# A causal convolution's set-up: sums formed while transposing on TensorE, two weights made off VectorE, and another order

## Chip, cores and metric

One core of one Trainium2 chip. The metric is the time of one execution on the device in microseconds; a number quoted for a kernel is the median of its runs. A kernel is called faster or slower when it differs by more than 2%, and "same" within that. Each experiment was timed in three rounds beside the kernel before on the same chip. The experiments ran on several chips; the kernel before had medians of 796.1 to 796.8 us on all of them, which links the sessions: the changed kernel was timed in another one. Where I set an experiment against it, I give the difference of the medians; by the two ratios to the kernel before, it comes out within 0.8 us of that.

## The reference

```python
# x [8, 4096, 512], kernel [8, 512, 512], both float32, drawn with a fixed seed
def reference(x, kernel):
    out = np.zeros_like(x)
    for k in range(8):
        shifted = x if k == 0 else concatenate([zeros(B, k, D), x[:, :-k, :]], axis=1)
        out += np.matmul(shifted, kernel[k])
    return out
```

Every output row is the sum of eight earlier rows of x, each times its own 512x512 matrix.

## The kernel before

The time axis is cut into 128 runs, one for each partition, and every run is computed in steps of 8 rows. A step needs its 8 rows of x and the 7 rows before them. Done directly it would be 64 products of a row with a tap (one of the eight 512x512 matrices). The kernel uses a three-level scheme with fewer products: each step has three nodes, LO, HI and MID, and each node has nine products of four matmuls of 128x512: three first ones, two called V and four called L. The price is that sums of rows (the "streams" D4, D41, D42, D421; for the MID node D1, D2, D21) and differences of weights are needed. There are 8 loaded weights and 19 differences, written W[a, b, c] with MID in one or more places.

```python
    def mid_a(b_, c_): tt(W[MID, b_, c_], W[HI, b_, c_], W[LO, b_, c_], SUB)   # tt is VectorE
    def mid_b(a, c_):  tt(W[a, MID, c_], W[a, HI, c_], W[a, LO, c_], SUB)
    def mid_c(a, b_):  tt(W[a, b_, MID], W[a, b_, LO], W[a, b_, HI], SUB)
```

In the steady state x is transposed by DMA. The first step is prepared by another way, and this is what the change touches: the rows of x and of history are transposed on TensorE, copied out by ScalarE, and then summed on VectorE. "History" is the 7 rows ahead of each run, taken from the run before.

```python
    nc.vector.memset(D421, 0.0)                     # history goes into D421
    xi = [load_x(0, 0)]                             # rows 0..3 of x
    for b in range(B):                              # eight history loads
        nc.gpsimd.dma_start(out=D421[b * G + 1:(b + 1) * G, 1:8],
                            in_=xr[b * G:(b + 1) * G - 1, RUN - 7:RUN, :])
    for tap in (6, 4, 7, 5):
        load_w(tap)
    xi.append(load_x(0, 1))                         # rows 4..7 of x
    for tap in (2, 0, 3, 1):
        load_w(tap)
    ...
        transpose_pe(T, xi[0], range(0, 4))         # 16 matmuls of 128x128
        transpose_pe(H, D421, range(0, 8))          # 32
        nc.scalar.copy(out=XT[:, 0:4], in_=T[:, 0:4])
        ...
        nc.scalar.copy(out=hs, in_=H[:, 4:8])
        tt(D4[:, 5:8], H[:, 1:4], hs[:, 1:4], ADD)  # first stream
        tt(D4[:, 0:4], hs, XT[:, 0:4], ADD)
        ...
        transpose_pe(T, xi[1], range(4, 8))         # the second half of x
        nc.scalar.copy(out=XT[:, 4:8], in_=T[:, 4:8])
        tt(F1[:, 0], hs[:, 3], XT[:, 0], ADD)       # third stream: six sums
        ...
        tt(F21, F2[:, 0:4], F2[:, 1:5], ADD)
        ...                                         # D4, D41, D42, D421 of HI
    ...                                             # 8 zero-fills of PSUM
    nodes = [node_a1(*order[0])]                    # the first large product
    node_a0u(nodes[0]); node_seed(nodes[0])
    node_v(nodes[0], 0); node_v(nodes[0], 1)        # V products and "corrections"
    for k, (i, a) in enumerate(order):
        node_l(cur, 0, LO); node_l(cur, 0, HI)      # L products
        ...
            if k == 0:  # five differences for the second node
                mid_b(HI, HI); mid_c(HI, LO); mid_b(HI, LO); mid_c(HI, MID); mid_c(HI, HI)
            else:       # nine differences for the third node
                mid_a(LO, HI); mid_a(HI, HI); mid_b(MID, HI); mid_a(LO, LO); mid_a(HI, LO)
                mid_b(MID, LO); mid_c(MID, MID); mid_c(MID, LO); mid_c(MID, HI)
```

(Cuts are marked with dots; calls are joined on one line here to save room.) The correction is one VectorE operation after each V product; the L products of a node can only start after it. A node's two corrections are therefore good landmarks: first, second and third corrections are those of the LO, HI and MID node of the first step.

Of the kernel before, what the change touches and what calls it, by code (L numbers as in the profile page):

```python
# [18 lines left out]
LO, HI, MID = 0, 1, 2  # L19
# [3 lines left out]
def kernel(  # L23
# [6 lines left out]
    nc = tc.nc  # L30
    B, S, D = x.shape
# [21 lines left out]

    ctx.enter_context(tc.manual_schedule())

    ident = spool.tile([P, P], bf, name="ident")
    make_identity(nc, ident)
    zero = spool.tile([P, D], bf, name="zero")
    nc.vector.memset(zero, 0.0)

    W = {}
    for a in (LO, HI, MID):
        for b_ in (LO, HI, MID):
# [9 lines left out]
    D21 = spool.tile([P, 4, D], bf, name="D21")  # L73
    D1 = spool.tile([P, 2, D], bf, name="D1")

    F2 = spool.tile([P, 5, D], bf, name="F2")
    F21 = spool.tile([P, 4, D], bf, name="F21")
    F1 = spool.tile([P, 2, D], bf, name="F1")
    F0 = spool.tile([P, D], bf, name="F0")
# [1 line left out]
    def tt(o, a, b, op):  # L81
        nc.vector.tensor_tensor(out=o, in0=a, in1=b, op=op)  # L82


    def load_x(i, h):
        xin = xpool.tile([P, 4, D], bf, name="xin")
        nc.gpsimd.dma_start(out=xin, in_=xr[:, K * i + 4 * h:K * i + 4 * h + 4, :])  # L87
        return xin
# [15 lines left out]
    def prep_d27():  # L104
        tt(D2[:, 0], XT[:, 5], XT[:, 7], ADD)
# [26 lines left out]



    nc.vector.memset(D421, 0.0)  # L135
    xi = [load_x(0, 0)]
    for b in range(B):
        nc.gpsimd.dma_start(out=D421[b * G + 1:(b + 1) * G, 1:8],
                            in_=xr[b * G:(b + 1) * G - 1, RUN - 7:RUN, :])

    def load_w(tap):
        n = K - 1 - tap
        nc.gpsimd.dma_start(out=W[n >> 2, n >> 1 & 1, n & 1], in_=kr[:, :, tap, :])  # L143

    def mid_a(b_, c_):
        tt(W[MID, b_, c_], W[HI, b_, c_], W[LO, b_, c_], SUB)

    def mid_b(a, c_):
        tt(W[a, MID, c_], W[a, HI, c_], W[a, LO, c_], SUB)

    def mid_c(a, b_):
        tt(W[a, b_, MID], W[a, b_, LO], W[a, b_, HI], SUB)

    for tap in (6, 4, 7, 5):
        load_w(tap)
    xi.append(load_x(0, 1))
    for tap in (2, 0, 3, 1):
        load_w(tap)

    with tc.tile_pool(name="t", bufs=1, space=PSUM) as tpool:  # L160
        H = tpool.tile([P, K, D], bf, name="hist")
        T = tpool.tile([P, K, D], bf, name="xt0")

        def transpose_pe(o, src, ts_):
            for t in ts_:
                for c in range(DC):
                    nc.tensor.transpose(o[:, t, c * P:(c + 1) * P],  # L167
                                        src[:, t % src.shape[1], c * P:(c + 1) * P], ident)

        transpose_pe(T, xi[0], range(0, 4))  # L170
        transpose_pe(H, D421, range(0, 8))
        nc.scalar.copy(out=XT[:, 0:4], in_=T[:, 0:4])
        nc.scalar.copy(out=F0, in_=T[:, 0])
        hs = D421[:, 4:8]
        nc.scalar.copy(out=hs, in_=H[:, 4:8])  # L175
        tt(D4[:, 5:8], H[:, 1:4], hs[:, 1:4], ADD)
        tt(D4[:, 0:4], hs, XT[:, 0:4], ADD)
        prep_d41(LO)
        mid_b(LO, HI)
        tt(D42[:, 7], D4[:, 5], D4[:, 7], ADD)  # L180
        prep_d42(LO)
        mid_c(LO, LO)
        prep_d421(LO)
        mid_b(LO, LO)
        mid_c(LO, MID)
        mid_c(LO, HI)
        transpose_pe(T, xi[1], range(4, 8))
        nc.scalar.copy(out=XT[:, 4:8], in_=T[:, 4:8])  # L188
        tt(F1[:, 0], hs[:, 3], XT[:, 0], ADD)
        tt(F1[:, 1], XT[:, 0], XT[:, 1], ADD)  # L190
        tt(F2[:, 0], hs[:, 1], hs[:, 3], ADD)
        tt(F2[:, 1:3], hs[:, 2:4], XT[:, 0:2], ADD)
        tt(F2[:, 3:5], XT[:, 0:2], XT[:, 2:4], ADD)
        tt(F21, F2[:, 0:4], F2[:, 1:5], ADD)
        prep_d4(HI)
        prep_d41(HI)
        prep_d42(HI)
        prep_d421(HI)
        prep_d27()
    xi = [load_x(1, 0), load_x(1, 1)]  # L200


    ppool = ctx.enter_context(tc.tile_pool(name="p", bufs=3, space=PSUM))
    qpool = ctx.enter_context(tc.tile_pool(name="q", bufs=1, space=PSUM))
    for k in range(4):
        pw = ppool.tile([P, 2, D], f32, name="pp") if k else qpool.tile([P, 2, D], f32, name="qq")
        for h in range(2):
            nc.tensor.matmul(pw[:, h], lhsT=ident, rhs=zero, start=True, stop=True)  # L208

    mpool = ctx.enter_context(tc.tile_pool(name="m", bufs=2))  # L210
    cpool = ctx.enter_context(tc.tile_pool(name="c", bufs=2))
# [12 lines left out]
    def streams(i, a):  # L224

        if a == MID and i == 0:
            return (F0, [F1[:, 0], F1[:, 1]], [F2[:, 1], F2[:, 3]],
                    [F21[:, j] for j in range(4)])
        if a == MID:
            return (XT[:, 0], [D1[:, 0], D1[:, 1]], [D2[:, 1], D2[:, 3]],  # L230
                    [D21[:, j] for j in range(4)])
        o = 4 * a
        return (D4[:, o], [D41[:, 2 * a], D41[:, 2 * a + 1]], [D42[:, o], D42[:, o + 2]],
                [D421[:, o + j] for j in range(4)])
# [4 lines left out]



    def node_a1(i, a):
        n = Node()
        n.i, n.a, n.s = i, a, streams(i, a)
        n.q = qpool.tile([P, 2, D], f32, name="qq")
        product(n.q[:, 1], n.s[1][1], W[a, MID, HI], True)
        nc.scalar.copy(out=n.q[:, 0], in_=n.q[:, 1])  # L247
        n.p = {}
        return n
# [4 lines left out]

    def node_seed(n):
        for b_ in range(2):
            n.p[b_] = ppool.tile([P, 2, D], f32, name="pp")
            if b_ == LO:
                nc.scalar.copy(out=n.p[b_][:, 1], in_=n.q[:, 1])  # L259
            else:  # L260
                nc.scalar.mul(out=n.p[b_][:, 1], in_=n.q[:, 1], mul=-1.0)  # L261
        n.dts = cpool.tile([P, D], f32, name="dts")
        nc.scalar.copy(out=n.dts, in_=n.q[:, 0])  # L263
# [40 lines left out]

    order = [(0, LO), (0, HI), (0, MID)]
    order += [(i, a) for i in range(1, NIT) for a in (MID, LO, HI)]
    nodes = [node_a1(*order[0])]
    node_a0u(nodes[0])
    node_seed(nodes[0])
    node_v(nodes[0], 0)  # L310
    node_v(nodes[0], 1)
    for k, (i, a) in enumerate(order):
        cur = nodes[k]
        stage = k % 3
# [5 lines left out]
        if k < 2:  # L320
            node_l(cur, 1, LO)
            node_l(cur, 1, HI)
            node_e(cur, 0)
            if k == 0:
                mid_b(HI, HI)
                mid_c(HI, LO)
                mid_b(HI, LO)
                mid_c(HI, MID)
                mid_c(HI, HI)
                nodes.append(node_a1(*order[1]))  # L330
            else:
                mid_a(LO, HI)
                mid_a(HI, HI)
                mid_b(MID, HI)
                mid_a(LO, LO)
                mid_a(HI, LO)
                mid_b(MID, LO)
                mid_c(MID, MID)
                mid_c(MID, LO)
                mid_c(MID, HI)  # L340
                nodes.append(node_a1(*order[2]))
            node_e(cur, 1)
        nxt = nodes[k + 1] if k + 1 < len(order) else None
        if nxt:
            node_a0u(nxt)
# [26 lines left out]
            prep_d4(LO if stage == 1 else HI)  # L372
        if k >= 2:
            node_l(cur, 1, HI)
        if 1 <= k and k + 2 < len(order):
            nodes.append(node_a1(*order[k + 2]))
        if k >= 2:
            node_e(cur, 1)
        if stage == 1 and more:
# [33 lines left out]
```

## Time and profile before

| | before |
|---|---|
| runs | 795.45, 796.1, 798.13 us |
| profiled span | 793.6 us |
| first correction starts | 38.55 us |
| second | 48.16 us |
| third | 61.89 us |
| from about 63 us | TensorE always busy, 7.78 us a node |

The page's line of busy times is the first thing to read; it gives for each engine the busy microseconds, the share of the span, and the number of instructions (PE is TensorE, PEld its weight loads, DVE VectorE, ACT ScalarE, POOL GpSimd).

```profile
PE 760.0 (96%) x3528; PEld 345.7 (44%) x3528; DVE 662.3 (83%) x762; ACT 277.6 (35%) x455; POOL 44.7 (6%) x86
```

TensorE is busy for 96%, so a change to anything but the start can't do much: 33.6 us of idle TensorE is all that there is, apart from matmuls that run at half rate (four large ones take 1.91 us from 32.25 on, eight take 1.89 from 34.87 on). The next rows are the VectorE timeline (start, duration, line, operation, tiles, and in brackets the idle time before the row with what ended it).

```profile
38.55 0.70 DVE L82 TENSOR_TENSOR pp<-dts,pp 128x512 f32<-128x512 f32 x1 [0.78 <-PE pp L217]
...
48.16 0.70 DVE L82 TENSOR_TENSOR pp<-dts,pp 128x512 f32<-128x512 f32 x1 [2.33 <-PE pp L217]
...
49.56 10.67 DVE L82 TENSOR_TENSOR w<-w,w 128x2048 bf16<-128x2048 bf16 x9
...
61.89 0.69 DVE L82 TENSOR_TENSOR pp<-dts,pp 128x512 f32<-128x512 f32 x1
```

The reader should see that VectorE hardly waits between its first sum at 18.4 us and the third correction, and that the nine differences alone are 10.67 us of it. One more view, the table of stretches, sums this up for exactly that piece (from the first sum to the third correction; columns PE, PEld, DVE, ACT, POOL busy us, then clock, DMA share, GB/s):

```profile
18.41:61.89 43.48, 28.09 (x119) 12.13 (x120) 39.87 (x44) 12.20 (x17) 1.20 (x3) 1.00 0.73 126
```

VectorE was busy for 39.87 of 43.48 us.

### The profile page before, as it was taken

Reading aid. Unit: us, or ns where it says so; the run is one execution under the profiler, and the core shown is the slowest. Engines: PE = TensorE matmul, PEld = TensorE weight load, DVE = VectorE, ACT = ScalarE, POOL = GpSimd, SP = SyncE. Lnnn points to the kernel's source line nnn. Section 1 sums busy time; section 2 is a strip of 40 time slices with the busy share of each in tenths; the row PEclk is TensorE's granted clock in tenths of the full one; section 3 lists DMA queues with packets and bytes.
Section 4 is the critical chain, followed back from the end, with each engine's and each line's share of the span. In section 5 each row is a group of like instructions: output and inputs, shape, how many; then the busy total and the mean of one; then the engine's idle time right before and its main releaser. Section 6 shows DMA issues by size and latency. Waiting matters only on the chain.

```text
span 793.6 us, 9335 instructions
## 1 busy us (share of the span) xinstructions
PE 760.0 (96%) x3528; PEld 345.7 (44%) x3528; DVE 662.3 (83%) x762; ACT 277.6 (35%) x455; POOL 44.7 (6%) x86
## 2 busy tenths in 40 slices
PE   2579999999999999999999999999999999999997
PEld 2224444444444444444444444444444444444443
DVE  1989898888888888889888888988888879888895
ACT  2233323333333333333333333333333333333332
POOL 6000000000000000000000000000000000000000
PEclk9999999999999999999999999999999999999999
DMA  9936777787878778778878877787778777878842
GB/s 153 209 52 177 186 173 178 169 203 167 206 160 188 170 175 183 188 172 189 192 164 176 188 193 169 182 176 176 175 188 207 156 190 171 174 188 184 192 137 121
DMA packets 161132, 138.83 MB, mean 175 GB/s; under 512 B 132296, under 2 KB 136392, under 8 KB 161088
## 3 DMA queue, kind: packets, MB, share of 16 engines
q1 hardware_dynamic: 147392, 99.63, 46.1%
q0 software_dynamic: 13696, 38.61, 30.4%
q8 instruction: 27, 0.44, 0.2%
q14 instruction: 17, 0.14, 0.1%
HBM read 77.22 MB, written 67.11 MB: 182 GB/s over the span
## 4 chain that ended last, share of the span: by engine, by line
PE 94%; DMA 2%; DVE 2%; ACT 1%; issue 0%; POOL 0%; ACTq 0%
PE pp L217 62%; PE qq L217 31%; DMA xin<-in_x_dram 2%; DVE w L82 1%; DMA D<-in_x_dram 1%; POOL w L143 0%; PE pp L208 0%; PE xt L167 0%; ACT XT L188 0%; DVE D L135 0%; ACT pp L259 0%; DVE y L82 0%; ACT qq L247 0%; PE qq L208 0%; DVE pp L271 0%
## 5 line engine op out<-in xcount | busy, mean ns | idle before, releaser
L217 PE MATMUL pp<-w,D 128*128 128x512 bf16 x2280 | 523.4, 379 | 1.4 <-ACT pp L259 1.3
L217 PEld LDWEIGHTS <-D 128*128 128x128 bf16 x3296 | 322.5, 98 | 394.5 <-issue 6.5
L217 PE MATMUL qq<-w,D 128*128 128x512 bf16 x1016 | 251.2, 380 | 1.4 <-ACT qq L247 1.4
L82 DVE TENSOR_TENSOR D<-D 128x1024 bf16<-128x1024 bf16 (+1 forms) x256 | 232.0, 947 | 0.1
L82 DVE TENSOR_TENSOR y<-pp,ms 128x1024 f32<-128x1024 f32 x124 | 151.4, 1221 | 47.9 <-PE pp L217 47.9
L82 DVE TENSOR_TENSOR D<-XT 128x2048 bf16<-128x2048 bf16 (+2 forms) x157 | 146.6, 950 | 7.6 <-DMA XT<-xin 6.3
L247 ACT COPY qq<-qq 128x512 f32<-128x512 f32 x96 | 54.7, 570 | 267.3 <-PE qq L217 267.3
L259 ACT COPY pp<-qq 128x512 f32<-128x512 f32 x96 | 54.7, 570 | 177.1 <-PE qq L217 172.7
L82 DVE TENSOR_TENSOR pp<-dts,pp 128x512 f32<-128x512 f32 x96 | 66.4, 692 | 51.5 <-ACT dts L263 47.2
L294 ACT COPY ms<-pp 128x1024 f32<-128x1024 f32 x62 | 63.0, 1016 | 34.2 <-PE pp L217 34.2
L87 POOL DMA_DIRECT2D xin<-in_x_dram x64 | 34.0, 532 | 699.0 <-DMA XT<-xin 688.1
L271 DVE SCALAR_TENSOR_TENSOR pp<-pp,dts 128x512 f32<-128x512 f32 x96 | 66.8, 695 | 3.6
L263 ACT COPY dts<-qq 128x512 f32<-128x512 f32 x96 | 58.2, 606 | 0.0
L261 ACT ACTIVATE pp<-qq 128x512 f32<-128x512 f32 x96 | 56.6, 590 | 0.1
L217 PE MATMUL qq<-w,XT 128*128 128x512 bf16 x124 | 31.8, 379 | 0.0
L82 DVE TENSOR_TENSOR w<-w,w 128x2048 bf16<-128x2048 bf16 x19 | 22.4, 1219 | 0.2
L167 PE MATMUL xt<-ident,xin 128*128 128x128 bf16 x32 | 3.8, 312 | 15.4 <-DMA xin<-in_x_dram 15.4
L217 PEld LDWEIGHTS <-XT 128*128 128x128 bf16 x124 | 12.1, 98 | 14.6
L82 DVE TENSOR_TENSOR D<-hist,D 128x1536 bf16<-128x1536 bf16 x1 | 1.0, 957 | 15.1 <-ACT D L175 15.1
L167 PEld LDWEIGHTS <-xin 128*128 128x128 bf16 x32 | 3.2, 146 | 15.7 <-DMA xin<-in_x_dram 15.7
L167 PE MATMUL hist<-ident,D 128*128 128x128 bf16 x32 | 3.8, 313 | 4.1 <-DMA D<-in_x_dram 4.1
L217 PEld LDWEIGHTS <-F 128*128 128x128 bf16 x36 | 3.3, 97 | 9.5 <-DVE w L82 4.8
(28 smaller groups left out, 51.4 us busy)
## 6 DMA issues: line engine op xcount, KB each, us to landing
out_dram<-y SPq DMA_DIRECT2D x128, 512.0 KB, 3.3
xin<-in_x_dram POOLq DMA_DIRECT2D x64, 512.0 KB, 6.0
w<-in_kernel_dram POOLq DMA_DIRECT2D x8, 512.0 KB, 13.9
XT<-xin SPq DMA_TRANSPOSE x62, 6.1
D<-in_x_dram POOLq DMA_DIRECT2D x8, 105.0 KB, 5.1
```

Of the source, the lines that this page charges most:

```text
L82: nc.vector.tensor_tensor(out=o, in0=a, in1=b, op=op)
L87: nc.gpsimd.dma_start(out=xin, in_=xr[:, K * i + 4 * h:K * i + 4 * h + 4, :])
L167: nc.tensor.transpose(o[:, t, c * P:(c + 1) * P], src[:, t % src.shape[1], c * P:(c + 1) * P], ident)
L217: nc.tensor.matmul(bank, lhsT=comp[:, c * P:(c + 1) * P], rhs=w[:, c, :], start=start and c == 0, stop=c == DC - 1, skip_group_check=True)
L247: nc.scalar.copy(out=n.q[:, 0], in_=n.q[:, 1])
L259: nc.scalar.copy(out=n.p[b_][:, 1], in_=n.q[:, 1])
L261: nc.scalar.mul(out=n.p[b_][:, 1], in_=n.q[:, 1], mul=-1.0)
L263: nc.scalar.copy(out=n.dts, in_=n.q[:, 0])
L271: nc.vector.scalar_tensor_tensor(out=p[:, 0], in0=p[:, 1], scalar=-1.0, in1=n.dts, op0=MUL, op1=SUB)
L294: nc.scalar.copy(out=ms[b_], in_=p)
```

## The change

The intent is to start the steady part earlier. A sum of transposed rows can be had from TensorE for nothing more than the transposes: a matmul of the row tile with an identity accumulates into PSUM, so two or four matmuls into the same place are a transposed sum. For history, an identity whose columns of the first run of each batch are zero does the masking, so history comes by two plain loads, and only one row of its tile has to be cleared. Two of the nine differences of the third node are made in the same way (identity times one weight plus minus-identity times the other) and copied out by ScalarE; two more of the nine move ahead of the second corrections. The second half of x is transposed only behind the first node's first three products. Sixteen zero-fills go to the front.

```diff
-    nc.vector.memset(D421, 0.0)
-    xi = [load_x(0, 0)]
-    for b in range(B):
-        nc.gpsimd.dma_start(out=D421[b * G + 1:(b + 1) * G, 1:8],
-                            in_=xr[b * G:(b + 1) * G - 1, RUN - 7:RUN, :])
+    nc.gpsimd.dma_start(out=H[1:P, 4:8], in_=xr[0:P - 1, RUN - 4:RUN, :])
+    x0 = [load_x(0, 0)]
+    nc.gpsimd.dma_start(out=H[1:P, 1:4], in_=xr[0:P - 1, RUN - 7:RUN - 4, :])
+    ...
+    nc.gpsimd.tensor_copy(out=identh, in_=ident)
+    nc.gpsimd.memset(identh[:, 0:P:G], 0.0)
+    nc.gpsimd.tensor_scalar_mul(out=identn, in0=ident, scalar1=-1.0)
...
+    def by_pe(o, u, v, prs):
+        for h in range(2):
+            pw = pair(prs[h])
+            for k in range(2):
+                nc.tensor.matmul(pw[:, k], lhsT=ident, rhs=u[:, 2 * h + k], start=True, stop=False)
+                nc.tensor.matmul(pw[:, k], lhsT=identn, rhs=v[:, 2 * h + k], start=False, stop=True)
+            nc.scalar.copy(out=o[:, 2 * h:2 * h + 2], in_=pw)
...
+    def sums_pe(k, *sums):
+        pw = pair(k)
+        for h, ts_ in enumerate(sums):
+            for c in range(DC):
+                for n, t in enumerate(ts_):
+                    src, idt = x_at(t)
+                    nc.tensor.matmul(pw[:, h, c * P:(c + 1) * P], lhsT=src[:, c * P:(c + 1) * P],
+                                     rhs=idt, start=n == 0, stop=n == len(ts_) - 1,
+                                     skip_group_check=True)
+        return pw
+
+    for r in range(2):
+        for k in range(4):
+            fill(pair(k))
+    o = transpose_pe(x0[0], 0)
+    nc.scalar.copy(out=XT[:, 0:4], in_=o)
+    pw = sums_pe(1, (-4, 0), (-3, 1))
+    nc.vector.tensor_copy(out=D4[:, 0:2], in_=pw)
+    ...                                   # the rest of D4
+    pw = sums_pe(1, (-1, 0), (0, 1))      # third stream, drained by ScalarE
+    nc.scalar.copy(out=F1, in_=pw)
+    ...                                   # F2 and F21 likewise
...
     node_seed(nodes[0])
+    o = transpose_pe(x0[1], 2)            # second half of x, now here
     node_v(nodes[0], 0)
     node_v(nodes[0], 1)
+    nc.scalar.copy(out=XT[:, 4:8], in_=o)
...
             if k == 0:
-                mid_b(HI, HI)
-                ...
+                by_pe(*mid_a(LO, HI), (2, 0))
+                node_e(cur, 1)
+                fill(pair(2))
+                nodes.append(node_a1(1))
+                by_pe(*mid_a(HI, HI), (1, 0))
+                prep_d421(HI)
+                ...                       # by_dve: six differences
             else:
-                mid_a(LO, HI)
-                ...
+                ...                       # by_dve: five differences
```

## The prediction

> **What bounds the kernel now.** I read the page first, then a table of busy time by stretch, then the chain that ended last in order of time, and last the timeline of the first 65 us.
>
> The table of stretches (engine: busy us and, in brackets, instructions; then granted clock, DMA share, GB/s):
>
> ```profile
> 0.00:20.00 20.00, 5.48 (x48) 4.95 (x48) 3.63 (x4) 5.50 (x4) 12.39 (x25) 1.00 0.99 154
> 20.00:40.00 20.00, 11.64 (x48) 5.41 (x49) 18.95 (x25) 4.01 (x5) 0.54 (x1) 1.00 1.21 210
> 40.00:60.00 20.00, 14.56 (x64) 5.90 (x63) 17.43 (x17) 7.54 (x11) 0.53 (x1) 1.00 0.28 47
> 60.00:80.00 20.00, 19.82 (x93) 8.86 (x92) 18.59 (x23) 7.54 (x13) 0.53 (x1) 1.00 0.72 183
> 100.00:400.00 300.00, 300.00 (x1391) 135.85 (x1390) 257.15 (x298) 107.38 (x179) 13.76 (x26) 1.00 0.78 180
> ```
>
> The columns are PE, PEld, DVE, ACT, POOL. From 60 us on TensorE is busy throughout; before that it waits. The diff touches only what happens before the third group of products, so everything at stake lies in the first 63 us. The steady part can't move: its 36 matmuls a node take 7.78 us by the chain, 216 ns each.
>
> The chain of those 63 us (start, us, what):
>
> ```profile
> 11.14 13.86 DMA xin<-in_x_dram
> 25.05 1.90 PE xt L167 x16
> 26.97 1.87 ACT XT L188
> 28.89 1.01 PE qq L208 x2
> 29.90 2.56 PE pp L208 x6
> 32.46 1.72 PE qq L217 x4
> ...
> 49.65 2.27 DVE w L82 x2
> ...
> 51.95 3.51 DVE w L82 x3
> ...
> 62.63 1.89 PE pp L217 x8
> ```
>
> The reader is to see two different bounds. Up to 32 us TensorE stands behind the second half of x: it lands at 25.0, sixteen transposes follow, ScalarE copies them out, only then is PSUM free for the zero-fills and the first product. From 49 us VectorE sets the pace with nine differences of weights (L82 w). The timeline shows that VectorE had begun late too, and that the matmul rate doubles on the way:
>
> ```profile
> 13.31 3.17 PE L167 MATMUL hist<-ident,D 128*128 128x128 bf16 x28 [4.11 <-DMA D<-in_x_dram]
> 16.51 1.87 ACT L175 COPY D<-hist 128x2048 bf16<-128x2048 bf16 x1 [5.35 <-PE hist L167]
> 18.41 0.96 DVE L82 TENSOR_TENSOR D<-hist,D 128x1536 bf16<-128x1536 bf16 x1 [15.13 <-ACT D L175]
> 32.25 1.91 PE L217 MATMUL qq<-w,D 128*128 128x512 bf16 x4
> 34.87 1.89 PE L217 MATMUL qq<-w,D 128*128 128x512 bf16 x8 [0.70 <-ACT qq L247]
> ```
>
> VectorE waited 15.1 us: history landed at 13.3, was transposed (3.2), copied (1.9), and only then added. The last two rows are the same instruction at about 0.43 and then 0.22 us apiece.
>
> [...] half rate until 34.2 us, 5.3 us after the fills began, full rate at 34.9. [...] The trace has only cold ones, 28 in 3.17 us, 113 ns apiece; halved that is 57 [...]. [...] the weight differences took 1219 ns here[...].
>
> **The change part by part.** Removed: the 1.77 us memset before the history loads, 32 history transposes, the 1.87 us copy, VectorE's 0.96 and 1.22 us sums for the first stream, and its six sums for the third (0.42 x 3 + 0.69 x 2 + 1.23 = 3.9 us). Two weight differences (2 x 1.22) leave VectorE for TensorE and ScalarE. Added: 152 matmuls of 128 columns, 16 more fills of 128x512 and 16 of 128x512 for the two weights. Moved: eight history transfers become two, one of them ahead of x; the second half's transposes go behind the first node's products; fills go to the front, where they only warm the array.
>
> I now walk the new order. Durations from the rows: difference or 4-row sum 1.22, 2-row sum 0.69, 1-row 0.42, ScalarE copy of 128x1024 1.02, of 128x512 0.57 to 0.61, of four rows of x 1.87, VectorE out of PSUM 1.22 for 1024 and 0.69 for 512, product (4 matmuls) 0.87 us.
>
> Arrivals: the old stream carried 210 GB/s once full, 0.524 MB in 2.5 us. The first issue is now at about 0.75. Estimated landings: history's upper rows 6.0, x 8.3, its lower rows 10.2, four weights 12.7 to 20.2, x's second half 22.7 (25.0 before), four weights 25.2 to 32.7.
>
> First node, at 62 ns: the identity is ready at about 3.1; sixteen fills, some twelve at 0.43 and four at 0.22, end near 9.2; transposes of x to 10.2; sums to 13.7, drained by VectorE from 11.3 to 14.4 and by ScalarE to 14.8. VectorE goes on: D41 15.1, D42 16.7, first difference 17.9, D421 19.2, four differences to 24.0. TensorE does the 96 sums of the third stream by 20.1; ScalarE drains the last at 21.2; fill, then first product 21.65 to 22.5 (32.25 before). ScalarE turn 0.7; eight matmuls to 25.0; x's second transposes to 26.0; two V products to 27.75; the two VectorE corrections end at 28.6.
>
> Second node: VectorE then has, in a row and without waits, D4, D41, a difference, D42, D421 (1.22 + 0.69 + 1.22 + 1.22 + 1.22), six differences (7.3) and D2 (0.42), ending at 41.7 to 41.9; the corrections end at 43.1. TensorE (by_pe, product, four V and L products) is ahead of that and waits for VectorE about 1.4 us. Third node: five differences (6.1), 1.85 for the next step's D1 and D2, the first correction at 51.7. The point that stood at 62.63 stands at about 52.3: 10.3 us earlier.
>
> [...] I put the gain between, leaning to the slow side for hand-overs that I did not count: 8.3 us. The weights on VectorE explain little of this alone: what it saves there is 2.4 + 3.9 us, but the gain comes mostly from its starting at 11 instead of 18.4 us.
>
> **The rivals.** First: TensorE becomes the bound of the set-up and stays cold. For it: it had no stretch of 128-column work in the fast state here, and 168 at 113 ns are 19 us, 8.6 more than at 62. Against it: sixteen fills give 6 us of dense work just ahead. It would leave about 2 us of gain, 794. Second: the transfers decide. The last weights land by my estimate at 32.7 and are first needed at 34.1, x's second half at 22.7 and 25.0; if the front were as slow as the 154 GB/s of the first 20 us, both would come some 3 us late and eat 1 to 2 us: 789. Third: the whole set-up hides nothing and the change gives the best that VectorE's own work allows. From its first copy at 11.3 its work to the last correction is about 37 us, so TensorE could go at some 49, a gain of 13 to 14: 782.5. Against it: VectorE must wait for the first node's V products, nearly 3 us. Fourth: the ScalarE copies stand in a queue in front of the seeds, and two copies per weight lie between the products of node two; I have them in the walk, with VectorE later than ScalarE there, so they are hidden unless a copy out of PSUM is slower than 1.02.
>
> **Range and chances.** 796.1 - 8.3 = 787.8. [...] a slower front or a late clock makes 790 to 791; hand-overs cheaper than I think make 785. The runs of before lie within 2.7 us. So 784.8 to 791.2 should hold it 8 times in 10. Two per cent is 15.9 us, more than even the bound from VectorE's work alone (13.6), so faster by 2% has 1%; slower by 2% would need the set-up to grow by a quarter, 1%.
>
> **What would show it.** In the profile after: the first large product at 21 to 25 us in place of 32.25; [...] VectorE's first copy near 11 us and its rows then without a long gap except about 3 us before the first corrections; L-products of the third node at 52 to 56 us; from there an unchanged 7.78 us a node. Wrong would be: sums at 110 ns and more, a wait for the history or for weights over 1 us on TensorE or VectorE, or steady-state waits that were not there before.

What stands is the walk at 62 ns, my estimate, a little above the halved cold row (57). It gives a gain of 10.3 us and so 796.1 - 10.3 = 785.8. The forecast takes 8.3 of it, 796.1 - 8.3 = 787.8: the 2.0 us between rest on the cut pace and on hand-overs that I did not count. They were not shown by any trace, nor was the upper end of the 52 to 56 us for the third node's L products.

## The result, and the profile after

| | before | after |
|---|---|---|
| runs | 795.45 to 798.74 us, median 796.43 (6) | 786.47 to 788.36 us, median 786.66 (6) |
| ratio | | 0.9877, 95% interval 0.986 to 0.9895 |
| profiled span | 793.6 | 784.6 |
| first correction | 38.55 | 27.65 |
| second | 48.16 | 42.57 |
| third | 61.89 | 52.18 |
| third node's eight L products start | 62.63 | 53.63 |

A ratio here is the mean time of one kernel's runs over that of the other's of the same rounds, so it is not quite the ratio of the medians that I quote. The gain is 9.8 us by medians, 1.2%, "same" by the 2% rule, and 786.66 is 1.1 us below the predicted 787.8. The page's busy times:

```profile
PE 769.1 (98%) x3680; PEld 352.0 (45%) x3680; DVE 658.2 (84%) x755; ACT 284.4 (36%) x463; POOL 42.7 (5%) x83
```

TensorE has 152 instructions more in the sum (152 small sums, 16 fills and 16 for the weights come, 32 transposes go) and is busy 9 us longer, yet the span is 9 us shorter: idle time was filled, the total work did not shrink. The table of stretches answers to the one in the prediction (columns as there):

```profile
0.00:20.00 20.00, 15.80 (x188) 11.73 (x189) 9.90 (x12) 7.67 (x7) 10.22 (x22) 1.00 0.98 166
20.00:40.00 20.00, 16.54 (x84) 7.43 (x84) 15.98 (x16) 11.63 (x16) 0.78 (x2) 1.00 1.15 202
40.00:60.00 20.00, 17.21 (x78) 7.60 (x78) 18.40 (x21) 7.41 (x13) 0.80 (x2) 1.00 0.48 103
...
100.00:400.00 300.00, 300.00 (x1391) 135.77 (x1390) 255.53 (x297) 107.62 (x180) 13.53 (x26) 1.00 0.79 180
```

The steady stretch is what it was: 1391 matmuls in 300 us in both kernels. The first 20 us show the move: TensorE from 5.48 to 15.80 us busy, VectorE from 3.63 to 9.90. The chain that ended last, in order of time (start, us, what):

```profile
4.58 9.40 DMA w<-in_kernel_dram
...
14.27 20.93 DMA w<-in_kernel_dram
35.29 1.24 DVE w L77
36.55 4.67 DVE w L77 x5
...
43.31 4.49 PE pp L251 x20
...
51.05 4.49 PE pp L251 x20
```

The second half of x is gone from the chain. In its place stands the stream of weight transfers, up to 35.29 us, and then VectorE with its differences. The timeline of TensorE shows the new front:

```profile
3.64 5.31 PE L184 MATMUL pp<-zero,ident 128*128 128x512 bf16 x16 [3.64 <-POOL ident masks.py:199]
9.33 1.07 PE L190 MATMUL pp<-ident,xin 128*128 128x128 bf16 x16 [0.39 <-DMA xin<-in_x_dram]
...
12.02 1.56 PE L203 MATMUL pp<-identh,D 128*128 128x128 bf16 x25
...
20.93 1.03 PE L251 MATMUL pp<-w,D 128*128 128x512 bf16 x4
...
53.63 1.89 PE L251 MATMUL pp<-w,F 128*128 128x512 bf16 x8
```

The 25 sums of the third row take 1.56 us from the first start to the last end; 0.22 us of that is one instruction's own duration, so they start (1.56 - 0.22) / 24 = 56 ns apart. The first large product is at 20.93 in place of 32.25. VectorE:

```profile
11.33 1.23 DVE L214 CAST D<-pp 128x1024 bf16<-128x1024 f32 x1 [8.08 <-PE pp L203]
...
19.68 1.23 DVE L77 TENSOR_TENSOR w<-w,w 128x2048 bf16<-128x2048 bf16 x1 [0.64 <-DMA w<-in_kernel_dram]
22.23 3.62 DVE L77 TENSOR_TENSOR w<-w,w 128x2048 bf16<-128x2048 bf16 x3 [1.31 <-DMA w<-in_kernel_dram]
27.65 0.69 DVE L77 TENSOR_TENSOR pp<-dts,pp 128x512 f32<-128x512 f32 x1 [1.81 <-PE pp L251]
...
35.29 7.03 DVE L77 TENSOR_TENSOR w<-w,w 128x2048 bf16<-128x2048 bf16 x6 [0.55 <-DMA w<-in_kernel_dram]
...
52.18 0.70 DVE L77 TENSOR_TENSOR pp<-dts,pp 128x512 f32<-128x512 f32 x1 [0.67 <-PE pp L251]
```

VectorE begins at 11.33 and now waits, for weights (0.64, 1.31, 0.55) and for V products (1.81, 0.67). The stretch from its first work on the streams to the third correction:

```profile
11.33:52.18 40.85, 34.42 (x266) 19.29 (x264) 35.29 (x37) 22.30 (x28) 3.09 (x5) 1.00 0.96 165
```

Set against the same stretch of before, this is a small account of the whole gain. VectorE starts 18.41 - 11.33 = 7.08 us earlier. It is busy 39.87 - 35.29 = 4.58 us less. It is idle 5.56 us in place of 3.61, which is 1.95 us more. 7.08 + 4.58 - 1.95 = 9.71 us, the shift of the third correction. It is an account up to that point and not quite of the end: behind it the changed kernel's TensorE has one more product ahead of its L products, which therefore come 9.00 us earlier (62.63 and 53.63), and by as much the two profiled executions differ (spans 793.6 and 784.6). The medians differ by 9.8 because the profiled execution of the kernel before is the fastest of its six.

### The profile page after: what moved, and what is told of

It reads as the page before. It is cut to its first block, busy times and chain, and to the rows that moved or that the text cites. A ratio compares the mean times of both kernels' runs of the same rounds, so it can differ in the third digit from the quotient of the medians.

```text
span 784.6 us, 9628 instructions
## 1 busy us (share of the span) xinstructions
PE 769.1 (98%) x3680; PEld 352.0 (45%) x3680; DVE 658.2 (84%) x755; ACT 284.4 (36%) x463; POOL 42.7 (5%) x83
## 4 chain that ended last, share of the span: by engine, by line
PE 92%; DMA 4%; DVE 2%; issue 1%; POOL 0%; ACT 0%; DVEq 0%; ACTq 0%; POOLq 0%
PE pp L251 92%; DMA w<-in_kernel_dram 4%; DVE w L77 1%; DVE y L77 1%; DVE D L77 0%; DVE pp L77 0%; ACT pp L295 0%; POOL D L136 0%; DVE pp L307 0%; ACT pp L283 0%; POOL D L138 0%; POOL identn L146 0%; POOL ident masks.py:199 0%; POOL identh L143 0%; POOL xin L82 0%
## 5 line engine op out<-in xcount | busy, mean ns | idle before, releaser
L251 PE MATMUL pp<-w,D 128*128 128x512 bf16 x3296 | 718.9, 379 | 3.9 <-DVE w L77 1.8
L283 ACT COPY pp<-pp 128x512 f32<-128x512 f32 x96 | 54.8, 571 | 260.1 <-PE pp L251 260.1
L295 ACT COPY pp<-pp 128x512 f32<-128x512 f32 x96 | 54.7, 570 | 175.9 <-PE pp L251 170.5
L299 ACT COPY dts<-pp 128x512 f32<-128x512 f32 x96 | 58.2, 606 | 0.0
L297 ACT ACTIVATE pp<-pp 128x512 f32<-128x512 f32 x96 | 56.6, 590 | 0.1
L251 PE MATMUL pp<-w,XT 128*128 128x512 bf16 x124 | 31.8, 379 | 0.0
L77 DVE TENSOR_TENSOR w<-w,w 128x2048 bf16<-128x2048 bf16 x17 | 20.2, 1221 | 2.8 <-DMA w<-in_kernel_dram 2.5
L184 PE MATMUL pp<-zero,ident 128*128 128x512 bf16 x24 | 7.7, 463 | 4.5 <-POOL ident masks.py:199 3.6
L251 PE MATMUL pp<-w,F 128*128 128x512 bf16 x36 | 8.7, 379 | 1.4 <-ACT pp L283 0.7
L203 PE MATMUL pp<-ident,xin 128*128 128x128 bf16 x80 | 7.5, 219 | 0.0
L203 PE MATMUL pp<-identh,D 128*128 128x128 bf16 x72 | 6.9, 219 | 0.0
L184 PEld LDWEIGHTS <-ident 128*128 128x128 bf16 x24 | 2.6, 116 | 8.3 <-issue 3.7
```

The source lines that it names most:

```text
L77: nc.vector.tensor_tensor(out=o, in0=a, in1=b, op=op)
L184: nc.tensor.matmul(pw[:, h], lhsT=ident, rhs=zero, start=True, stop=True)
L203: nc.tensor.matmul(pw[:, h, c * P:(c + 1) * P], lhsT=src[:, c * P:(c + 1) * P], rhs=idt, start=n == 0, stop=n == len(ts_) - 1, skip_group_ ...
L251: nc.tensor.matmul(bank, lhsT=comp[:, c * P:(c + 1) * P], rhs=w[:, c, :], start=start and c == 0, stop=c == DC - 1, skip_group_check=True)
L283: nc.scalar.copy(out=n.q[:, 0], in_=n.q[:, 1])
L295: nc.scalar.copy(out=n.p[b_][:, 1], in_=n.q[:, 1])
```

## The experiments

My theory after the result was that several things had to come off the path together: the late second half of x ahead of the first product, the third stream's sums on VectorE, and two differences on VectorE. If that holds, undoing any one of them must cost a large part of the gain, and doing one alone must give little. The first rival was that one part does nearly all. The second rival was that transfers decide now, so that the parts on VectorE hardly count. All diffs are against the changed kernel unless another is named. None of these kernels, except one that says so, gives a wrong result.

### weights_vector: the two weights back on VectorE

```diff
             if k == 0:
-                by_pe(*mid_a(LO, HI), (2, 0))
                 node_e(cur, 1)
                 fill(pair(2))
                 nodes.append(node_a1(1))
-                by_pe(*mid_a(HI, HI), (1, 0))
...
                 by_dve(*mid_c(HI, HI))
+                by_dve(*mid_a(LO, HI))
+                by_dve(*mid_a(HI, HI))
                 by_dve(*mid_b(MID, HI))
```

> The changed kernel with its two differences of weights back on VectorE (two more rows of 1.22 us, just ahead of the differences that need them), TensorE's 16 products of 128x512 and ScalarE's four copies for them gone. Theory A (VectorE sets the pace from the first node's corrections at 29 us to the third node's at 52 us): 1.8 to 2.4 us slower than the changed kernel, about 788.8; the 0.67 us that VectorE waits for TensorE before the third node's correction is the only slack. Rival (ScalarE's copies and TensorE's extra products hold the second node, so taking them away pays for the VectorE rows): 0 to 0.5 us, about 787.

Measured: 789.96 us (789.22 to 791.03), ratio 0.9927 [0.991, 0.9943]. The timeline of VectorE:

```profile
35.03 9.42 DVE L77 TENSOR_TENSOR w<-w,w 128x2048 bf16<-128x2048 bf16 x8 [0.20 <-DMA w<-in_kernel_dram]
```

Eight differences in 9.42 us where there were six in 7.03: 2.39 us. The wait before them was shorter by 0.35, and the third node's L products start at 55.77, 2.14 later than in the changed kernel. That is the expectation. The medians differ by 3.3 us. Two of the four runs, the profiled one among them, are 2.6 us above the changed kernel; the other two are 4.0 and 4.4 above it, and of them I have no trace. So about 2.1 us are shown, and the rest of the runs' difference stays open.

### third_vector: the third stream's sums back on VectorE

```diff
-    pw = sums_pe(1, (-1, 0), (0, 1))
-    nc.scalar.copy(out=F1, in_=pw)
+    pw = sums_pe(1, (-4,), (-3,))          # history rows transposed alone
+    nc.scalar.copy(out=hs[:, 0:2], in_=pw)
...
-    pw = sums_pe(0, (-3, -2, -1, 0), (-2, -1, 0, 1))
-    nc.scalar.copy(out=F21[:, 0:2], in_=pw)
...
     by_dve(*mid_c(LO, HI))
+    tt(F1[:, 0], hs[:, 3], XT[:, 0], ADD)
+    ...                                    # the six sums of the kernel before
+    tt(F21, F2[:, 0:4], F2[:, 1:5], ADD)
```

> The changed kernel with the third stream's sums back on VectorE: TensorE transposes four history rows alone (32 matmuls of 128 columns with the masked identity in place of 96), ScalarE copies them, and VectorE makes six sums (3.9 us) after the first node's weights, where it now waits 1.8 us for the first V product. Theory A: 3.9 - 1.8 = 2.1 us slower, 788.8. Rival B (TensorE's sums and ScalarE's drains are what the first node waits for): no slower, even faster, 786 or less, since 64 matmuls and two drains go away. If the transfers of the weights set the first node (theory C) the first product comes earlier but the second ones do not, and the loss is again 2.1.

Measured: 788.89 us (788.44 to 789.48), ratio 0.9909 [0.9895, 0.9924], 2.2 us slower, as expected. The first correction went from 27.65 to 30.75, the third from 52.18 to 54.42. The six sums lie there from 26.92 to 30.46, 3.5 us, and 1.5 of it falls into the wait for the V product, which shrank from 1.81 to 0.29. The other 1.1 of the first correction's delay is the fourth weight, which was used at 23.38 in place of 22.23 in this execution, for a reason that I don't know; 0.55 of it comes back where the changed kernel waits for its last weight. A line that I had not asked for:

```profile
24.66 3.60 PE L254 MATMUL pp<-w,D 128*128 128x512 bf16 x8 [2.56 <-DVE w L78]
```

Eight large matmuls take 3.60 us, at half the rate of 1.89 elsewhere. With the small matmuls of the third stream gone, TensorE waited (3.59 us before the first product, 2.56 before these eight), and its clock fell: the mean granted clock of the first 60 us is 0.91, against 1.00 in the changed kernel.

### x_second_early: the second half of x ahead of the first product again

```diff
     nc.scalar.copy(out=F0, in_=XT[:, 0])
+    o = transpose_pe(x0[1], 2)
+    nc.scalar.copy(out=XT[:, 4:8], in_=o)
     fill(pair(0))
...
     node_seed(nodes[0])
-    o = transpose_pe(x0[1], 2)
     node_v(nodes[0], 0)
     node_v(nodes[0], 1)
-    nc.scalar.copy(out=XT[:, 4:8], in_=o)
```

> The changed kernel with the transposes and the copy of x's second half put back ahead of the first product, as they stood before. They can't start until it lands, by the order of the transfers at about 24.8 us. Theory A: the first product moves from 20.9 to some 26.5 us and the first corrections from 27.65 to about 31, minus what VectorE then no longer waits for the copy: 2.5 to 3.5 us slower, 789.5 to 790. Rival (the first node is held by the weights, and this order costs nothing): under 0.7 us.

Measured: 792.76 us (791.91 to 793.09), ratio 0.9956 [0.9941, 0.9971]: 6.1 us slower, twice what I expected. TensorE's timeline, then VectorE's:

```profile
25.63 1.89 PE L190 MATMUL pp<-ident,xin 128*128 128x128 bf16 x16 [6.07 <-DMA xin<-in_x_dram]
...
34.44 0.69 DVE L77 TENSOR_TENSOR pp<-dts,pp 128x512 f32<-128x512 f32 x1 [7.71 <-PE pp L253]
```

After a wait of 6.07 us the transposes take 1.89 us in place of 1.07, and the fills behind them 0.43 us apiece. The half landed at 25.6, 0.8 later than I had put it. From that landing to the first correction are 8.81 us. Of the 6.1, then, 0.8 is a landing that I had too early, and some of the rest could be the cold clock; two later runs test this.

### order_alone: the kernel before with only this one move

The diff is against the kernel before. PSUM is divided into fixed pairs, as in the changed kernel, because otherwise the transposes hold the banks (in the kernel before the fills wait 1.95 us until ScalarE has copied them out).

```diff
-        transpose_pe(T, xi[1], range(4, 8))
-        nc.scalar.copy(out=XT[:, 4:8], in_=T[:, 4:8])
...
     node_seed(nodes[0])
+    o = transpose_pe(2, x01)
     node_v(nodes[0], 0)
     node_v(nodes[0], 1)
+    nc.scalar.copy(out=XT[:, 4:8], in_=o)
+    xi.append(load_x(1, 1))
+    ...                                    # D4, D41, D42, D421 of HI
+    fill(2)
```

> The kernel before with one thing moved: the transposes and the copy of x's second half go behind the first node's first products (and the zero fills therefore ahead, with PSUM in fixed pairs). Sums, weights, history transfers and their order stay as before; all differences of weights on VectorE. Theory A: VectorE still starts at 18.4 us and still does all its work, so only 1 to 3 us of the 9.8 come: 793.5 to 795.5. Rival B (the order is most of the gain): 7 us or more, 789 or less.

Measured: 797.44 us (795.63 to 797.51), ratio 1.0011 [0.9996, 1.0026] to the kernel before. A clear miss: nothing was gained. First comes the table of stretches for the first 60 us, of this kernel and then of the changed one; the number after the five engines is the granted clock:

```profile
0.00:60.00 60.00, 35.89 (x156) 16.71 (x157) 38.70 (x42) 16.02 (x18) 13.47 (x27) 0.82 0.80 137
```

```profile
0.00:60.00 60.00, 49.55 (x350) 26.77 (x351) 44.28 (x46) 26.71 (x33) 11.80 (x25) 1.00 0.87 157
```

and the timeline of the former, TensorE and VectorE:

```profile
42.28 3.59 PE L213 MATMUL pp<-w,D 128*128 128x512 bf16 x8 [1.25 <-DVE w L82]
46.58 7.76 PE L213 MATMUL pp<-w,D 128*128 128x512 bf16 x24 [0.71 <-ACT pp L256]
...
48.56 0.70 DVE L82 TENSOR_TENSOR pp<-dts,pp 128x512 f32<-128x512 f32 x1 [3.94 <-PE pp L213]
```

The first correction did come earlier, at 32.74 in place of 38.55. But the second stood at 48.56 (before: 48.16), because TensorE then computed the second node at half rate, and VectorE waited 3.94 us for it. What the move won was lost again to the clock. The clock column alone does not show every slow matmul: it reads 1.00 for the first 20 us of the kernel before, where sixteen transposes take 1.89 us against 1.07 in the changed kernel. So the durations have to be read beside it.

### order_warm: the same with zero-fills in TensorE's waits

To test that reading, order_alone was given extra matmuls of zeros into free banks, which compute nothing that is used. The diff is against order_alone.

```diff
-    for k in (3, 0, 1, 2):
+    for k in (3,) * 8 + (0, 1, 2):
         fill(k)
...
     nodes = [node_a1(*order[0])]
+    for r in range(8):
+        fill(2)
...
                 mid_c(HI, HI)
+                for r in range(4):
+                    fill(2)
                 nodes.append(node_a1(*order[1]))
+                for r in range(2):
+                    fill(2)
...
                 nodes.append(node_a1(*order[2]))
+                for r in range(5):
+                    fill(1)
```

> The kernel with the order alone moved, plus zero fills of banks that are free at that time, put where TensorE would wait (16 products ahead of the first product, 16 ahead of the next two, 12 around the second node's first, 10 in the third node). They do no work. In the order-alone run the first node's corrections came 5.8 us earlier than before, yet the second node's no earlier (48.56 against 48.16), with TensorE at about 0.43 us a product: theory, the waits let the clock fall to half and that ate the gain. Then this run gains 2.5 to 4 us over the kernel before, 792.5 to 793.7. Rival (the order gains nothing because VectorE sets the end whatever the clock): 796, no gain.

Measured: 793.79 us (793.01 to 794.49), ratio 0.9966 [0.995, 0.9982] to the kernel before: 2.7 us faster than before by the ratio, and 3.6 faster than order_alone by medians, as expected.

```profile
45.81 5.49 PE L213 MATMUL pp<-w,D 128*128 128x512 bf16 x24 [0.71 <-ACT pp L256]
...
46.94 0.70 DVE L82 TENSOR_TENSOR pp<-dts,pp 128x512 f32<-128x512 f32 x1 [1.78 <-PE pp L213]
```

The 24 matmuls that took 7.76 us take 5.49, the mean granted clock of the first 60 us is 1.00 in place of 0.82, and the second correction comes at 46.94. So the cold clock is shown to be what ate the move's gain. The changed kernel does not need such fills: its 152 sums and 16 matmuls for the two weights are the filling (where third_vector takes 64 of the sums away, and weights_vector the 16 matmuls, eight large matmuls at half rate appear: 3.60 and 3.57 us, at a mean granted clock of 0.91 and 0.94 in the first 60 us).

These rows do not show which wait costs the rate; its length alone does not tell. In one_weight_pool a wait of 1.73 us was followed by four large matmuls in 1.04 us and then four in 1.86; in two_weights_pool one of 1.89 us at the same place was followed by 1.04 and 1.02.

### x_early_warm and x_early_warm_short: the same test from the other side

To x_second_early, fills were added in the 6 us wait for the second half of x: 28 matmuls in the first, 16 in the second.

```diff
     nc.scalar.copy(out=F0, in_=XT[:, 0])
+    for r in range(14):        # x_early_warm; range(8) in x_early_warm_short
+        fill(pair(3))
+    o = transpose_pe(x0[1], 2)
+    nc.scalar.copy(out=XT[:, 4:8], in_=o)
```

> The changed kernel with x's second half transposed ahead of the first product, as in the run that cost 6 us, plus 28 zero fills of a free bank in TensorE's 6 us wait for that half. That run's timeline has the transposes, the four fills and the first product at half rate after the wait: 1.89 - 1.06, 1.88 - 1.02 and part of the product, some 2 us. Clock theory: 2 us of the 6 come back, 4 us slower than the changed kernel, about 790.7. Rival (the 6 us are the landing and the ScalarE copy alone): no change from 792.8.

Measured: 793.51 us (793.37 to 794.24), ratio 0.9955 [0.9935, 0.9975]: a miss, and no better than x_second_early. TensorE's timeline says why:

```profile
19.99 8.36 PE L184 MATMUL pp<-zero,ident 128*128 128x512 bf16 x26 [0.27 <-PE pp L203]
```

I had counted 0.22 us a fill. They took 8.36 / 26 = 0.32 on average. Both fills of a round go into one pair of banks, and the next round asks for the same pair again; their weight loads come two at a time, 0.65 us from one two to the next, with 0.34 us idle in between. In the changed kernel's front, where the fills go round four pairs, the last seven start 0.22 us apart. So the fills ended at 28.3, and held back the transposes of data that in the neighbouring runs had landed at 24.8 to 25.6. From there to the first correction it was 7.22 us in place of 8.81, so the effect was there, but the overshoot took more. Sixteen fit (the next text's "two fills of one bank" are fills of the two banks of one pair):

> The run with 28 zero fills in TensorE's wait overshot: two fills of one bank after the other took 0.32 us each there, so that they ended at 28.2 us, 2.6 us after x's second half had landed; but from the first transpose to the first correction it then took 7.22 us against 8.81 without fills. Here 16 fills, which should end at some 25.1 us. Clock theory: the transposes start at about 25.6 at full rate, the first correction comes at about 32.9 in place of 34.44, and 1.5 us of the 6 come back, 791.2. Rival: no better than the 792.8 without fills.

Measured: 791.16 us (791.02 to 791.57), ratio 0.9936 [0.9919, 0.9953], as expected.

```profile
24.79 1.07 PE L190 MATMUL pp<-ident,xin 128*128 128x128 bf16 x16 [0.35 <-DMA xin<-in_x_dram]
```

The transposes are at full rate, and from the first of them to the first correction (32.02) it takes 7.23 us against 8.81. These 1.58 us don't depend on when the half landed (24.8 here, 25.6 there), and the medians differ by 1.6 as well. x_second_early's loss of 6.1 us is thus about 1.6 from the cold clock and 4.5 from the order itself.

### no_front_fills: without the sixteen fills at the front

```diff
-    for r in range(2):
-        for k in range(4):
-            fill(pair(k))
     o = transpose_pe(x0[0], 0)
```

> The changed kernel without the sixteen zero fills at its front; nothing reads what they write. Clock theory: the transposes and some 30 to 60 of the sums then run at 113 ns in place of 56 until TensorE is at full rate; VectorE's first copies come 1.5 to 2 us later, but the wait for the third and fourth weight (2 us in all) swallows that on VectorE, and the end of the sums delays the first product: 0.5 to 2 us slower, about 788. Rival (transposes and sums never bring the full rate by themselves): all sums at 113 ns, first product some 8 us later, 5 us or more slower, about 792. Second rival (the transfers decide the whole first node): under 0.4 us.

Measured: 787.09 us (786.87 to 787.25), ratio 0.9882 [0.9867, 0.9896]: 0.4 us slower, which the intervals don't tell from nothing. The fills do what they are for, as the same transposes and the first VectorE row show:

```profile
9.41 1.89 PE L190 MATMUL pp<-ident,xin 128*128 128x128 bf16 x16 [9.41 <-DMA xin<-in_x_dram]
...
13.05 1.23 DVE L211 CAST D<-pp 128x1024 bf16<-128x1024 f32 x1 [9.80 <-PE pp L203]
```

VectorE starts 1.72 us later, and still the end moves by at most 0.5. The wait for the fourth weight shrinks from 1.31 to 0.53, and the wait of 0.64 for the third is gone. An early start was given back in waits for weights: 0.78 + 0.64 of the 1.72. TensorE's later start still made the first correction 1.0 late (28.66), but the wait of 0.55 for the last weight is gone as well, and the third correction stands at 52.53, 0.35 later. This is the first sign that the front of VectorE's work has slack. Of the expectations, the first rival falls: behind 16 transposes and some 30 sums at 107 ns apart, the sums are at full rate from 14.3 us on, without any fill. Between the clock theory (0.5 to 2 us) and the second rival (under 0.4) a loss of 0.4 does not decide.

### weights_late and no_history: are the transfers the bound?

In weights_late the second half of x is loaded ahead of the third and fourth weights; these come one transfer later. In no_history the two history loads are left out and the tile is cleared instead, so that all later transfers come earlier by 0.9 MB. This kernel's result is wrong on purpose (relative error 0.114), and it shows only the time.

```diff
-    for tap in (6, 4, 7, 5):
+    for tap in (6, 4):
         load_w(tap)
     x0.append(load_x(0, 1))
+    for tap in (7, 5):
+        load_w(tap)
```

```diff
-    nc.gpsimd.dma_start(out=H[1:P, 4:8], in_=xr[0:P - 1, RUN - 4:RUN, :])
     x0 = [load_x(0, 0)]
-    nc.gpsimd.dma_start(out=H[1:P, 1:4], in_=xr[0:P - 1, RUN - 7:RUN - 4, :])
...
-    nc.vector.memset(H[0:1], 0.0)
+    nc.vector.memset(H, 0.0)
```

> The changed kernel with the load of x's second half moved two places up, ahead of the third and fourth weight, which then land about 2.5 us later; every other landing stays. Transfer theory (the fourth weight's landing at 22.2 us sets the first node: VectorE waited 1.3 us for it): 2.5 us slower, 789.2, up to 4 if TensorE's longer wait lets its clock drop. Rival (VectorE's own work or TensorE's sums set the first node and the weights have slack): under 0.5 us.

Measured: 790.54 us (790.32 to 790.84), ratio 0.9926 [0.9911, 0.994]: 3.9 us slower. Timeline of VectorE and TensorE:

```profile
22.43 1.23 DVE L77 TENSOR_TENSOR w<-w,w 128x2048 bf16<-128x2048 bf16 x1 [3.21 <-DMA w<-in_kernel_dram]
...
26.29 3.47 PE L253 MATMUL pp<-w,D 128*128 128x512 bf16 x8 [3.94 <-DVE w L77]
```

The wait for the third weight is 3.21 in place of 0.64, so 2.57 us come from the transfer, which is one transfer's time in the stream (the changed kernel's third and fourth weights come 2.55 us apart, at 19.68 and 22.23). Behind it TensorE waited 3.94 us and lost its clock: eight matmuls in 3.47 instead of 1.89, 1.58 us. 2.57 + 1.58 = 4.15, and the first correction moved from 27.65 to 31.62, 3.97; the third moved by 3.32, after the wait for the last weight had gone.

> A wrong result on purpose: the changed kernel without its two history loads (the history is zero in every row), 0.89 MB less ahead of the weights, so that everything lands about 4.3 us earlier, and TensorE's start about 1.1 us earlier since two issues less stand before the identity. Transfer theory: VectorE's 2.5 us of waits for weights go too, first corrections at about 25 in place of 27.65, in all 3 us faster than the changed kernel, 783.6. Rival (only the front of TensorE and VectorE counts): 1.1 to 1.5 us faster, 785.3.

Measured: 784.37 us (783.25 to 785.8), ratio 0.9843 [0.9823, 0.9863]: 2.3 us faster by medians, between the two expectations. No wait for a weight is left, and the first correction is at 25.96 and the third node's L products at 51.30, 2.33 earlier. (The profiled execution, the slowest of the four, keeps this lead up to its last correction and loses 1.4 us behind it.) So the transfers are on the path, by about 2.3 us, of which some 0.4 is not the weights' but x's: TensorE's transposes start at 8.95 in place of 9.33. They show no wait for x and stand right behind the sixteen fills at the front, which take 6.59 us here (0.41 apiece), so they might have started sooner, and 2.3 is by my estimate rather too little. With them away the first node is set by TensorE: VectorE waits 2.87 us for the first V product instead of 1.81.

### one_weight_pool and two_weights_pool: differences on GpSimd

From 29 to 52 us VectorE is the bound, so I tried to take one or two more differences off it. GpSimd was nearly idle there (in the changed kernel 0.78 us busy from 20 to 40 us).

```diff
+    def by_pool(o, u, v):
+        nc.gpsimd.tensor_tensor(out=o, in0=u, in1=v, op=SUB)
...
-                by_dve(*mid_a(LO, LO))
+                by_pool(*mid_a(LO, LO))
...
-                by_dve(*mid_a(HI, LO))      # only in two_weights_pool
+                by_pool(*mid_a(HI, LO))
```

> The changed kernel with one difference of weights (the low-low one of the third node, the last but one ahead of the second node's corrections) moved from VectorE to GpSimd, which is idle from 27 us on. VectorE then has one row of 1.22 us less ahead of its corrections; the first V product of that node is there at 41.2 us, so the corrections can come 1.2 us sooner, at 41.4, and the third node follows by as much: 1.2 us faster than the changed kernel, 785.5, if GpSimd reads SBUF beside VectorE freely. Rival [...]: VectorE's rows of that stretch get longer than 1.22 us by as much as GpSimd takes, and the time stays or grows, 786.7 to 789.

Measured: 790.51 us (790.36 to 792.23), ratio 0.9922 [0.9896, 0.9948]: 3.9 us slower than the changed kernel by medians. Timelines of GpSimd and of VectorE:

```profile
32.77 4.15 POOL L168 TENSOR_TENSOR w<-w,w 128x2048 bf16<-128x2048 bf16 x1 [3.24 <-DMA w<-in_kernel_dram]
...
32.92 5.08 DVE L77 TENSOR_TENSOR w<-w,w 128x2048 bf16<-128x2048 bf16 x1
```

The VectorE difference that lay beside GpSimd's took 5.08 us in place of 1.22: VectorE stood nearly still for as long as GpSimd worked. This costs 3.86 and saves 1.22. In the profiled execution a second loss came first: the first correction was at 29.66, 2.0 later than in the changed kernel, before GpSimd had computed anything: one product's four matmuls and the sixteen transposes behind them ran at half rate (1.86 us each in place of 1.02 and of 1.06, 1.6 us together), and the fourth weight was used 0.4 later. From the first to the third correction it took 26.40 us, against 24.53: 1.9 us is what GpSimd's help itself cost.

> As the run with one weight on GpSimd, and the high-low difference of the third node there too. Free case: VectorE loses another 1.22 us after the second node's corrections, but there TensorE's chain of product, copy, products is only 0.67 us behind it, so almost nothing is added: 785 to 785.5. Shared case: VectorE slows for twice as long, or waits for GpSimd's second result before its next difference: 788 or more.

Measured: 794.24 us (793.39 to 795.24), ratio 0.9963 [0.9941, 0.9985], 7.6 us slower.

```profile
32.93 9.93 POOL L168 TENSOR_TENSOR w<-w,w 128x2048 bf16<-128x2048 bf16 x2 [4.93 <-DMA w<-in_kernel_dram]
...
32.74 6.22 DVE L77 TENSOR_TENSOR D<-D 128x2048 bf16<-128x2048 bf16 x2
38.88 9.73 DVE L77 TENSOR_TENSOR w<-w,w 128x2048 bf16<-128x2048 bf16 x5
```

Two VectorE sums took 6.22 (2.48 otherwise) and five differences 9.73 (5.88 otherwise): 7.59 us more, for 9.93 us of GpSimd's work. Here the first node stayed at full rate (first correction 28.14), so in these rows the slowing is seen alone. What follows is mixed again: TensorE waited 5.82 us for VectorE, lost its rate (the next eight matmuls took 3.60 us), and VectorE waited 0.50 us for it in turn, and 1.73 before the third correction.

No correct kernel of these beat the changed one; only no_front_fills comes level with it.

## Why the prediction was right

**The size.** 787.8 was predicted and 786.66 measured, inside the range. The route was right as well: the landmarks of the walk at 62 ns lie within 1 us of the measured ones almost everywhere. Of its own signs, though, not all came out: a wait for weights over 1 us was to count as wrong, and VectorE waited 1.31 us for the fourth; the first product (20.93) came just ahead of its 21 to 25 us, and the sums (56 ns apart) were faster than the 62 of its walk.

| landmark, us | predicted | measured |
|---|---|---|
| VectorE's first copy | 11.3 | 11.33 |
| first large product | 21.65 | 20.93 |
| third weight's difference begins | no wait | 19.68, after a wait |
| first node's corrections end | 28.6 | 29.15 |
| second corrections end | 43.1 | 43.9 |
| third correction | 51.7 | 52.18 |
| third node's L products | 52.3 in the walk at 62 ns, 52 to 56 as a sign | 53.63 |

**The pace of the small matmuls** was mis-sized. I worked with 62 ns and with a slower pace, and leaned to the slow side; the sums start 56 ns apart, the prediction's own alternative of the halved cold row (57). That this alternative fits so well is luck: its 113 ns include the last matmul's own 0.31 us, and start to start the cold ones are 107 ns apart. At 56 ns the walk gives 168 x 6 ns = 1.0 us more than its 10.3, a gain of 11.3; the third node's L products came 9.0 us earlier. What is missing, 2.3, is also the size of the next point, though no run shows that it is the same 2.3.

**The landings** were estimated too early. x landed at 9.3, not 8.3, and the third and fourth weights at about 19.7 and 22.2, not 17.7 and 20.2. The second rival, that transfers decide, was therefore partly true: it eats 2.3 us of what was possible (no_history), and a transfer more costs 3.9 (weights_late). It is smaller than it might have been because TensorE comes next, close behind. The two errors, a pace too slow and landings too early, have opposite signs, which is part of why the sum came out so near. That part is luck.

**What set the first rival aside** was right but for too small a reason. I argued that the fills at the front would warm the array. They do, but no_front_fills shows this to be worth 0.4 us at most. What counts in these runs is that TensorE has something to do in the later waits. The prediction never named this, and it is the largest thing that it missed: order_alone lost 3.6 us to the clock, and half-rate matmuls stand in x_second_early (four fills in 1.88 us), third_vector (eight matmuls in 3.60) and weights_late (eight in 3.47) too. (weights_vector has eight of them, 3.57 us, but there VectorE came later anyway.)

**"The gain comes mostly from its starting at 11 instead of 18.4 us"** was too strong. By the account above the early start is 7.08 us, of which 1.95 is given back as waits, and 4.58 us is less work. At the margin an early start is worth even less: 1.72 us of it cost 0.4 (no_front_fills). The prediction's saving of 2.4 + 3.9 us of rows left out the two-sided trade in the first stream: 2.2 us of sums go, 3.1 us of copies out of PSUM come.

**The parts don't add up singly.** Undoing one costs 6.1 (order), 2.2 (third stream) and 3.3 us by medians (weights, 2.1 by its trace), 11.6 in all, more than the whole gain of 9.8, and the first stream's sums and the fewer history loads are not in it. Doing the order alone gave nothing, and with a warm clock 2.7. This is what the theory of parts that must come together says, and the rival of one part doing nearly all falls for the order. The other parts were only undone and never tried alone on the kernel before.

**The third rival**, the best that VectorE's work allows (782.5), was not reached: VectorE is idle for 5.56 us in the stretch, 4.98 of it in the five waits for weights and for V products above.

Left open: the gain of the first stream's sums and of the merged history loads by themselves, which no run isolates, and 1 us of weights_vector's runs beyond its trace. Nor is it shown why a wait of 1.73 us cost the clock in one_weight_pool, while one of 1.89 in two_weights_pool at the same place did not.

## What to carry to other kernels

An engine that waits in a set-up can take work from the one that sets the pace, and on TensorE such small work also kept the matmul rate up here for the large work after it (eight large matmuls took 1.04 + 1.02 us behind it, 3.60 in third_vector without part of it); so when work is taken off TensorE, or a wait is moved, look at the matmul durations before and behind the wait, not only at its length. Before an engine's start is pulled forward, look at what it will wait for next: here 1.7 us of earlier start was worth under half a microsecond. An idle engine isn't a free one (beside GpSimd's 4.15 us a VectorE difference took 5.08 in place of 1.22): try one instruction on it and read the rows of its neighbour.
